# Down projection of a hybrid block: residual read by ScalarE's queue, four value buffers, rows ended one by one, norm weight before the norm

## The chip, the cores and the metric

The kernel runs on one core of one Trainium2 chip. TensorE multiplies matrices into PSUM banks, VectorE and ScalarE work element by element, GpSimd does some sums and stores, and SyncE, ScalarE and GpSimd issue DMAs between HBM and SBUF. Each engine takes its own instructions strictly in order and waits for the others by semaphores. The metric is the device time of one execution in microseconds. Before the change it is 1729.08 us, the median of three runs (1724.63 to 1731.36).

## The reference

A decoder block over 1024 tokens of 1024 channels, all in float32: two attention mixers, gates and an output projection, then a SwiGLU feed-forward of width 2816, and a last RMS norm. The change touches only the end, from the feed-forward's second product on:

```python
u = rms_norm(h, ffn_norm_g[layer])
h = h + swiglu(u, w_gate[layer], w_up[layer], w_down[layer])   # silu(u@w_gate) * (u@w_up) @ w_down
return rms_norm(h, final_norm_g)      # h * rsqrt(mean(h*h) + 1e-6) * final_norm_g
```

## The kernel before

**Products.** The down projection multiplies gated values (1024 tokens by 2816) by `w_down` (2816 by 1024). Both are cut into two by two blocks and multiplied with seven block products instead of eight (Strassen's method in Winograd's form), named in `PRODUCTS`: A00, S1, S2, S4, S3, A01, A11. Each runs over 11 blocks of 128 rows, so there are 77 steps. I number them 0 to 76, with step n = 11 i + p for product i and block p.

**One step.** A step needs a value tile (128x512, read back from HBM, where the feed-forward's first half left it: `fetch`) and a weight tile (128x512, in SBUF; in some products it is first made as a difference of two). Float32 is kept by splitting each into a rounded part and a rest (`split`): ScalarE casts the rounded part `oh`, VectorE subtracts it to get the rest `ol`. TensorE then does three products (L1372 to L1374) for each of four blocks of 128 tokens (`tb`), 12 matmuls of 128x512 a step. Four PSUM banks gather one product, one bank for each `tb`; two sets, `bx` and `by`, take turns. In the trace the banks of `bx` are called tp, tp, mm, mm.

**Rings.** The value tiles have a ring of two, `ar`; `oh` and `ol` have rings of six each, shared with the feed-forward's first half, which is three steps of two. A value buffer is free again when VectorE has taken the rest from it.

**Order.** The Python loop fetches step n+2, prepares step n+1 and multiplies step n. The instructions then pass a scheduler that gives each engine a fixed order of its own. On SyncE's queue it puts the eight reads of the residual (`hf`, 512 KB each, L1417) and eleven reads of weight blocks (`b10`, 256 KB each, L1289) among the first values of product A00, because their buffers are free by then.

**Ends.** When a product is complete its banks are kept (`kept`) or added to the residual rows `hf[t]` and squared (`settle`: t is one of eight blocks of 128 rows, c one of two halves of 512 columns). When both halves of `hf[t]` are complete, `finish` adds the two sums of squares, takes the reciprocal root (L168 to L181, with the root itself on ScalarE, L172), multiplies each half by the root and by the norm's weight in one VectorE instruction (L1400, L1402) and stores it. Rows t = 0 to 3 end after product A01, t = 4 to 7 at the very end. The last three steps (74 to 76) are written so that each `tb` runs through all three and is then settled:

```python
elif n == NS - 1:
    for tb in range(4):
        for m in range(NS - GRP, NS):
            step(m, (tb,))
        settle(tb + 4, 0, bx[tb], None)
        finish(tb + 4)
```

With rings of six the operands of step 76 can be cast only when step 73 is done, and the scheduler laid these steps out one after the other, all four banks in each.

## Time and profile before

| | |
|---|---|
| median of three runs | 1729.08 us |
| profiled execution, whole time | 1729.99 us |
| its span, first to last instruction | 1728.3 us |
| TensorE busy | 1648.4 us, 95% |
| VectorE busy | 1088.0 us, 63% |
| ScalarE busy | 769.7 us, 45% |
| GpSimd busy | 441.9 us, 26% |
| mean granted TensorE clock | 0.983 of full speed |

The busy share is an average over the whole run. The page's second part cuts the span into 40 slices of 43 us: TensorE reads 9 (90% or more) in nearly all of them, except the first, the 25th, the 36th (1512 to 1556 us) and the last, and these dips are where an engine waits for another. TensorE's records overlap: a 128x512 matmul is shown with 0.39 us, but the next one starts 0.23 us later. Idle time of an engine other than the one that is waited for costs nothing. The span leaves out 1.69 us that lie around it in the whole time.

### The profile page before, as it was taken

To read this page: it belongs to the slowest core of one execution; us is meant where nothing else is said; L and a number is where in the kernel's file an instruction comes from. 1 tells how busy PE (TensorE), PEld (TensorE's weight loads), DVE (VectorE), ACT (ScalarE), POOL (GpSimd) and SP (SyncE) were. 2 spreads that over 40 slices of the span, in tenths; PEclk is the share of its full clock that TensorE was granted. 3 is DMA by queue.
4 is the path that set the end of the run, shared out by engine and by line. 5 is a ranking of instruction groups with operands and counts; after the bars stand their busy time and mean duration, and the time that the engine had idled before them with its cause. 6 is when DMAs were issued, how large, how long until landed. Compare 5 with 4: busy or idle time off the path is not lost.

```text
span 1728.3 us, 25058 instructions
## 1 busy us (share of the span) xinstructions
PE 1648.4 (95%) x9025; PEld 1422.4 (82%) x9025; DVE 1088.0 (63%) x2148; ACT 769.7 (45%) x1644; POOL 441.9 (26%) x626
## 2 busy tenths in 40 slices
PE   5999999999999999999999997999999999989997
PEld 4888888888889988998878885788888888878885
DVE  8554545546349668888754248665655665766557
ACT  4334334334423257877854134433333333335444
POOL 4532323323122336656626110010010011100000
PEclk8999999999999999999999998999999999999998
DMA  6120211113213010100193420433223233763334
GB/s 209 46 80 25 80 43 44 49 44 95 85 71 99 17 31 12 49 16 20 29 313 125 167 98 37 134 123 122 92 97 116 92 103 105 253 231 95 98 97 146
DMA packets 150635, 163.68 MB, mean 95 GB/s; under 512 B 11616, under 2 KB 114048, under 8 KB 150512
## 3 DMA queue, kind: packets, MB, share of 16 engines
q1 hardware_dynamic: 139568, 129.62, 23.9%
q0 software_dynamic: 9760, 31.94, 4.8%
q8 instruction: 71, 1.16, 0.3%
q10 hardware_dynamic: 1184, 0.53, 0.1%
q14 instruction: 52, 0.43, 0.1%
HBM read 117.76 MB, written 44.30 MB: 94 GB/s over the span
## 4 chain that ended last, share of the span: by engine, by line
PE 80%; DVE 8%; issue 5%; ACT 3%; DMA 3%; POOL 2%; SPq 0%; DVEq 0%; ACTq 0%; POOLq 0%
PE mm L1140 8%; PE mm L1141 8%; PE mm L1142 8%; PE b L159 5%; PE b L160 5%; PE b L161 5%; PE b L927 3%; PE s L874 3%; PE mm L1372 3%; PE mm L1373 3%; PE mm L1374 3%; PE b L938 3%; PE s L159 2%; PE s L160 2%; PE s L161 2%
## 5 line engine op out<-in xcount | busy, mean ns | idle before, releaser
L1133 ACT ACTIVATE oh<-S 128x512 fp32r<-128x512 f32 x88 | 55.7, 633 | 138.9 <-PE mm L1141 138.3
L159 PE MATMUL b<-uh,mg_h 128*128 128x512 f32 x288 | 114.9, 399 | 0.7 <-ACT mg_st L337 0.7
L160 PE MATMUL b<-ul,mg_h 128*128 128x512 f32 x288 | 113.8, 395 | 0.0
L161 PE MATMUL b<-uh,mg_l 128*128 128x512 f32 x288 | 112.9, 392 | 0.0
L874 PE MATMUL s<-kN,qN 128*128 128x320 f32 (+5 forms) x384 | 98.8, 360 | 4.2 <-ACT p L891 3.3
L942 DVE TENSOR_TENSOR pl<-b,ph 128x512 fp32r<-128x512 f32 (+1 forms) x152 | 90.6, 613 | 12.3 <-ACT ph L941 11.2
L1351 ACT ACTIVATE oh<-ar 128x512 fp32r<-128x512 f32 x77 | 48.6, 632 | 106.5 <-PE mm L1373 72.8
L1352 DVE TENSOR_TENSOR ol<-ar,oh 128x512 fp32r<-128x512 f32 x77 | 53.3, 692 | 66.2 <-ACT oh L1351 62.6
L160 PE MATMUL b<-pw_l,uh 128*128 128x384 f32 x256 | 88.1, 344 | 6.5 <-DVE pw_l L269 6.5
L941 ACT ACTIVATE ph<-b 128x512 fp32r<-128x512 f32 (+1 forms) x152 | 80.2, 544 | 31.3 <-PE b L938 29.9
L891 ACT ACTIVATE p<-s,mn 128x640 f32<-128x640 f32 (+7 forms) x128 | 89.3, 703 | 7.6 <-DVE mn L885 2.5
L159 PE MATMUL b<-pw_h,uh 128*128 128x384 f32 x256 | 89.2, 348 | 1.8 <-ACT uh L218 1.2
L898 POOL TENSOR_TENSOR p<-p,sm 128x640 f32<-128x640 f32 (+3 forms) x64 | 89.2, 1414 | 2.5
L1133 ACT ACTIVATE oh<-raw 128x512 fp32r<-128x512 f32 x66 | 41.5, 632 | 108.3 <-PE mm L1141 104.7
L161 PE MATMUL b<-pw_h,ul 128*128 128x384 f32 x256 | 87.9, 343 | 1.4 <-DVE ul L219 1.4
L1373 PE MATMUL mm<-ol,oh 128*128 128x512 f32 x220 | 86.2, 392 | 0.0
L1374 PE MATMUL mm<-oh,ol 128*128 128x512 f32 x220 | 86.1, 391 | 0.0
L938 PE MATMUL b<-ident,p 128*128 128x128 f32 x528 | 82.5, 273 | 1.8 <-POOL p L895 1.2
L465 DVE TENSOR_REDUCE mn<-s 128x1 f32<-128x128 f32 (+7 forms) x64 | 46.0, 753 | 53.8 <-PE s L464 53.8
L1134 DVE TENSOR_TENSOR ol<-S,oh 128x512 fp32r<-128x512 f32 x88 | 59.6, 687 | 29.9 <-ACT oh L1133 25.6
L159 PE MATMUL s<-pw_h,uh 128*128 128x256 f32 (+1 forms) x256 | 75.9, 297 | 2.6 <-ACT xs L648 1.6
L927 PE MATMUL b<-ph,vN 128*128 128x256 f32 x264 | 75.1, 302 | 0.0
(432 smaller groups left out, 5188.9 us busy)
## 6 DMA issues: line engine op xcount, KB each, us to landing
raw<-in_w_gate_dram SPq DMA_DIRECT2D x22, 512.0 KB, 5.0
raw<-in_w_up_dram SPq DMA_DIRECT2D x22, 512.0 KB, 4.6
mg_raw<-in_w_in_dram SPq DMA_DIRECT2D x18, 512.0 KB, 4.6
mgd<-mg_st POOLq DMA_DIRECT2D x32, 256.0 KB, 3.7
sg<-mgd SPq DMA_DIRECT2D x16, 512.0 KB, 4.7
pw_raw<-in_w_in_dram SPq DMA_DIRECT2D x24, 256.0 KB, 4.2
b<-in_w_down_dram SPq DMA_DIRECT2D x22, 256.0 KB, 5.8
xt<-in_x_dram SPq DMA_DIRECT2D x8, 512.0 KB, 5.4
```

Of the source, the lines that this page charges most:

```text
L159: T.matmul(ps, ah, bh, start=(i == 0), stop=False)
L160: T.matmul(ps, ah, bl, start=False, stop=False)
L161: last = T.matmul(ps, al, bh, start=False, stop=(i == n - 1))
L874: T.matmul(s_[:, c], qN[:, 2 * hp + es[c * len(es) // 2], i * 128:(i + 1) * 128], kNs[br][:, v, g, c0:c0 + cw], start=(v == 0), stop=(v == 1))
L927: T.matmul(o, lhsT, rhs, start=(done == 0), stop=(done == total - 1))
L938: T.transpose(tp[:, 2 * (b - b0) + e], p[:, e, b * 128:(b + 1) * 128], ident)
L1133: A.activation(wh, src, AF.Copy)
L1140: T.matmul(ps, w[0][:, k], b[0][:, k], start=(first and k == 0), stop=False, **kw)
L1141: T.matmul(ps, w[0][:, k], b[1][:, k], start=False, stop=False, **kw)
L1142: T.matmul(ps, w[1][:, k], b[0][:, k], start=False, stop=(k == 3), **kw)
L1373: T.matmul(ps, ah[:, ts], wl, start=False, stop=False, **kw)
L1374: T.matmul(ps, al[:, ts], wh, start=False, stop=(p == HF - 1), **kw)
```

## The change

Four things are changed in the down projection, as the diff shows.

1. The residual's rows `hf[t]` are read by ScalarE's queue, one behind a value cast of steps 12, 14, 16 and 18 (t = 0 to 3) and 34, 36, 38 and 40 (t = 4 to 7). The norm's weight `gO` is read there behind the cast of step 23. `issue_after` fixes that place in ScalarE's order.
2. Values alternate between `ar` and two buffers `arf` in the memory of the feed-forward's raw weights, so a ring of four. Fetches run four steps ahead, preparing two.
3. The operands of step 73 go to four tiles of another ring, `u2d`, whose values are used up by then; so those of steps 74 to 76 fit into the rings of six together.
4. `settle` multiplies the rows by the norm's weight after they have been squared; `finish` has only the reciprocal root left, on VectorE for the first half and on ScalarE for the second.

```diff
@@ -1342,24 +1342,37 @@
         i, p = divmod(n, HF)
         if PRODUCTS[i][3]:
             load_block(PRODUCTS[i][3], p)
-        raw_a[n] = dn.tile([128, 512], F32, name="ar", bufs=2)
+        if n % 2:
+            raw_a[n] = ffr.tile([128, 512], F32, name="arf", tag="raw", bufs=2)
+        else:
+            raw_a[n] = dn.tile([128, 512], F32, name="ar", bufs=2)
         nc.sync.dma_start(raw_a[n], hh_dram[PRODUCTS[i][0]][p])
 
-    def split(src):
-        h = ff.tile([128, 512], R, name="oh", bufs=6)
-        l = ff.tile([128, 512], R, name="ol", bufs=6)
-        A.activation(h, src, AF.Copy)
+    def split(src, spare):
+        if spare:
+            h, l = [dr.tile([128, 512], R, name="u2" + v, tag="u2d", bufs=4) for v in "hl"]
+        else:
+            h = ff.tile([128, 512], R, name="oh", bufs=6)
+            l = ff.tile([128, 512], R, name="ol", bufs=6)
+        cast = A.activation(h, src, AF.Copy)
         V.tensor_sub(l, src, h)
-        return h, l
+        return (h, l), cast
 
     def prepare(n):
         i, p = divmod(n, HF)
         _, nm, make, _, _ = PRODUCTS[i]
-        a = split(raw_a.pop(n))
+        a, cast = split(raw_a.pop(n), n == NS - 1 - GRP)
         w = BW[nm][p]
         if make:
             V.tensor_sub(w, BW[make[0]][p], BW[make[1]][p])
-        ops[n] = a + split(w)
+        ops[n] = a + split(w, n == NS - 1 - GRP)[0]
+        if i in (1, 3) and 1 <= p < 9 and p % 2:
+            t = p // 2 + (0 if i == 1 else 4)
+            with tc.issue_after(cast.ins):
+                nc.scalar.dma_start(hf[t], hx_dram[t])
+        elif i == 2 and p == 1:
+            with tc.issue_after(cast.ins):
+                nc.scalar.dma_start(gO, bcast_rows(final_norm_g, D))
 
     def step(n, tbs):
         i, p = divmod(n, HF)
@@ -1391,32 +1404,29 @@
             V.tensor_add(hc, hc, part)
         sq = ff.tile([128, 512], F32, name="S", bufs=3)
         A.activation(sq, hc, AF.Square, accum_out=ssq[:, t, c:c + 1])
+        V.tensor_mul(hc, hc, gO[:, c * 512:c * 512 + 512])
 
     def finish(t):
         V.tensor_add(ssq[:, t, 0:1], ssq[:, t, 0:1], ssq[:, t, 1:2])
         r = rsqrt(dr, [128, 1], ssq[:, t, 0:1], 1.0 / D, "fin")
         rows = slice(t * 128, (t + 1) * 128)
         h0, h1 = hf[t][:, 0:512], hf[t][:, 512:1024]
-        V.scalar_tensor_tensor(h0, h0, r, gO[:, 0:512], op0=OP.mult, op1=OP.mult)
+        V.tensor_scalar(h0, h0, r, None, op0=OP.mult)
         nc.sync.dma_start(out[rows, 0:512], h0)
-        V.scalar_tensor_tensor(h1, h1, r, gO[:, 512:1024], op0=OP.mult, op1=OP.mult)
+        A.activation(h1, h1, AF.Copy, scale=r)
         nc.sync.dma_start(out[rows, 512:1024], h1)
 
-    for n in range(2):
+    for n in range(4):
         fetch(n)
     prepare(0)
+    prepare(1)
     keep = {}
     for n in range(NS):
         i, p = divmod(n, HF)
+        if n + 4 < NS:
+            fetch(n + 4)
         if n + 2 < NS:
-            fetch(n + 2)
-        if n == HF:
-            nc.sync.dma_start(gO, bcast_rows(final_norm_g, D))
-        if i in (2, 4) and p < 4:
-            t = p + (0 if i == 2 else 4)
-            nc.sync.dma_start(hf[t], hx_dram[t])
-        if n + 1 < NS:
-            prepare(n + 1)
+            prepare(n + 2)
         if n < NS - GRP:
             step(n, range(4))
         elif n == NS - 1:
```

**SyncE's queue, the values of steps 7 to 10.** `ar` and `arf` are value tiles (A00d_11162 is step 7, A00d_11163 step 8, A00d_11165 step 10), `hf` the residual's rows, `b` the weight blocks. Before:

```order
L1417 DMA hf_15391<-hxd_11233 128x1024
L1346 DMA ar<-A00d_11162 128x512
L1417 DMA hf_15392<-hxd_11234 128x1024
L1417 DMA hf_15393<-hxd_11235 128x1024
L1417 DMA hf_15394<-hxd_11236 128x1024
L1417 DMA hf_15395<-hxd_11237 128x1024
L1417 DMA hf_15396<-hxd_11238 128x1024
L1417 DMA hf_15397<-hxd_11239 128x1024
L1289 DMA b_0_15379<-in_w_down_dram 128x512
L1346 DMA ar<-A00d_11163 128x512
```

Now:

```order
L1349 DMA ar<-A00d_11163 128x512
L1289 DMA b_0_15379<-in_w_down_dram 128x512
L1289 DMA b_1_15380<-in_w_down_dram 128x512
L1349 DMA arf<-A00d_11164 128x512
L1289 DMA b_2_15381<-in_w_down_dram 128x512
L1289 DMA b_3_15382<-in_w_down_dram 128x512
L1289 DMA b_4_15383<-in_w_down_dram 128x512
L1289 DMA b_5_15384<-in_w_down_dram 128x512
L1289 DMA b_6_15385<-in_w_down_dram 128x512
L1289 DMA b_7_15386<-in_w_down_dram 128x512
L1289 DMA b_8_15387<-in_w_down_dram 128x512
L1349 DMA ar<-A00d_11165 128x512
```

The reads of the residual are gone from this queue; step 8's values (the first row) stand ahead of all weight blocks, step 9's behind two of them and step 10's behind nine.

**TensorE's and VectorE's last work.** The banks tp_15399, tp_15400, mm_15401 and mm_15402 belong to the rows hf4 to hf7. Operands 17245 and 17240 are step 74's, 17266 and 17261 step 75's and 17287 and 17282 step 76's in the new order; 17275 and 17270 are step 76's in the old. TensorE's last twelve matmuls before:

```order
L1372 MATMUL tp_15399<-oh_17275,oh_17270 128x512
L1372 MATMUL tp_15400<-oh_17275,oh_17270 128x512
L1372 MATMUL mm_15401<-oh_17275,oh_17270 128x512
L1372 MATMUL mm_15402<-oh_17275,oh_17270 128x512
L1373 MATMUL tp_15399<-ol_17276,oh_17270 128x512
L1374 MATMUL tp_15399<-oh_17275,ol_17271 128x512
L1373 MATMUL tp_15400<-ol_17276,oh_17270 128x512
L1374 MATMUL tp_15400<-oh_17275,ol_17271 128x512
L1373 MATMUL mm_15401<-ol_17276,oh_17270 128x512
L1374 MATMUL mm_15401<-oh_17275,ol_17271 128x512
L1373 MATMUL mm_15402<-ol_17276,oh_17270 128x512
L1374 MATMUL mm_15402<-oh_17275,ol_17271 128x512
```

Now:

```order
L1385 MATMUL mm_15401<-oh_17287,oh_17282 128x512
L1386 MATMUL mm_15401<-ol_17288,oh_17282 128x512
L1387 MATMUL mm_15401<-oh_17287,ol_17283 128x512
L1385 MATMUL mm_15402<-oh_17245,oh_17240 128x512
L1386 MATMUL mm_15402<-ol_17246,oh_17240 128x512
L1387 MATMUL mm_15402<-oh_17245,ol_17241 128x512
L1385 MATMUL mm_15402<-oh_17266,oh_17261 128x512
L1386 MATMUL mm_15402<-ol_17267,oh_17261 128x512
L1387 MATMUL mm_15402<-oh_17266,ol_17262 128x512
L1385 MATMUL mm_15402<-oh_17287,oh_17282 128x512
L1386 MATMUL mm_15402<-ol_17288,oh_17282 128x512
L1387 MATMUL mm_15402<-oh_17287,ol_17283 128x512
```

Before, the last twelve matmuls are step 76 on all four banks. Now the bank of hf6 is complete nine matmuls before the end, and only the bank of hf7 is worked on after that (of hf4 and hf5, 17 and 15 before the end). VectorE before, from the first row that waits for the last matmuls:

```order
L1388 TENSOR_TENSOR hf4_15394<-hf4_15394,tp_15399 128x512
L1388 TENSOR_TENSOR hf5_15395<-hf5_15395,tp_15400 128x512
L1388 TENSOR_TENSOR hf6_15396<-hf6_15396,mm_15401 128x512
L1388 TENSOR_TENSOR hf7_15397<-hf7_15397,mm_15402 128x512
L1396 TENSOR_TENSOR ssq_15398<-ssq_15398 128x1 x2
L168 TENSOR_SCALAR fin_a_17292<-ssq_15398 128x1
L168 TENSOR_SCALAR fin_a_17318<-ssq_15398 128x1
L1396 TENSOR_TENSOR ssq_15398<-ssq_15398 128x1 x2
L173 RECIPROCAL fin_r_17293<-fin_t_17294 128x1
```

Now, up to the row behind the last bank's addition:

```order
L1401 TENSOR_TENSOR hf6_15396<-hf6_15396,mm_15401 128x512
L1407 TENSOR_TENSOR hf5_15395<-hf5_15395,qB22l_15378 128x512
L1410 TENSOR_TENSOR ssq_15398<-ssq_15398 128x1
L168 TENSOR_SCALAR fin_a_17305<-ssq_15398 128x1
L173 RECIPROCAL fin_r_17306<-fin_t_17307 128x1
L1407 TENSOR_TENSOR hf6_15396<-hf6_15396,qB22l_15378 128x512
L168 TENSOR_SCALAR fin_a_17332<-ssq_15398 128x1
L1410 TENSOR_TENSOR ssq_15398<-ssq_15398 128x1
L176 SCALAR_TENSOR_TENSOR fin_t_17307<-fin_r_17306,fin_a_17305 128x1
L1401 TENSOR_TENSOR hf7_15397<-hf7_15397,mm_15402 128x512
L173 RECIPROCAL fin_r_17333<-fin_t_17334 128x1
```

The addition of hf7 stands behind the weight's multiplication of hf6 (L1407), and the reciprocal roots of hf4 and hf5 are worked out around it.

**ScalarE's casts of steps 71 to 73.** The names with 17169 and 17174 are step 71's before, with 17171 and 17176 now. Before, steps 71 to 73 follow in turn:

```order
L1351 ACTIVATE oh_17169<-ar_17144 128x512
L1351 ACTIVATE oh_17174<-b00_5_12214 128x512
L172 ACTIVATE fin_t_17046<-ssq_15398,epst_86 128x1
L1351 ACTIVATE oh_17192<-ar_17167 128x512
L1351 ACTIVATE oh_17197<-b00_6_12215 128x512
L172 ACTIVATE fin_t_17064<-ssq_15398,epst_86 128x1
L1351 ACTIVATE oh_17215<-ar_17190 128x512
L1351 ACTIVATE oh_17220<-b00_7_12216 128x512
```

Now u2h are the casts of step 73:

```order
L1357 ACTIVATE oh_17171<-arf_17123 128x512
L1357 ACTIVATE oh_17176<-b00_5_12214 128x512
L172 ACTIVATE fin_t_17051<-ssq_15398,epst_86 128x1
L1357 ACTIVATE u2h_17217<-arf_17169 128x512
L1357 ACTIVATE u2h_17222<-b00_7_12216 128x512
L1357 ACTIVATE oh_17194<-ar_17146 128x512
L1357 ACTIVATE oh_17199<-b00_6_12215 128x512
```

The casts of step 73 stand ahead of those of step 72.

## Rows read from the trace of the kernel before

**Rows 1.** Stages: busy us of PE, PEld, DVE, ACT, POOL; clock, DMA share, GB/s.
```profile
1500.00:1530.00 30.00, 25.06 (x100) 20.23 (x100) 20.49 (x34) 7.67 (x13) 3.24 (x6) 0.90 1.02 389
1530.00:1560.00 30.00, 30.00 (x131) 24.74 (x131) 23.71 (x38) 15.57 (x28) 0.00 (x0) 0.98 0.35 105
...
1620.00:1650.00 30.00, 30.00 (x134) 24.87 (x133) 18.85 (x30) 15.43 (x30) 0.00 (x0) 1.00 0.32 97
```

**Rows 2.** TensorE's timeline around 1520 us: start, length, line, tiles, [idle].
```profile
1519.32 0.39 PE L1373 MATMUL mm<-ol,oh 128*128 128x512 f32 x1
1519.55 0.39 PE L1374 MATMUL mm<-oh,ol 128*128 128x512 f32 x1
1524.88 1.22 PE L1372 MATMUL tp<-oh 128*128 128x512 f32 x2 [4.94 <-ACT oh L1351]
...
1531.51 0.39 PE L1373 MATMUL tp<-ol,oh 128*128 128x512 f32 x1
```

**Rows 3.** ScalarE's timeline: the last raw weights' cast, those of steps 7 and 8.
```profile
1481.72 0.63 ACT L1133 ACTIVATE oh<-raw 128x512 fp32r<-128x512 f32 x1 [1.19 <-DMA qB11h<-in_w_down_dram]
...
1514.39 0.63 ACT L1351 ACTIVATE oh<-ar 128x512 fp32r<-128x512 f32 x1 [4.31 <-PE mm L1373]
...
1523.67 0.63 ACT L1351 ACTIVATE oh<-ar 128x512 fp32r<-128x512 f32 x1 [8.13 <-DMA ar<-A00d]
```

**Rows 4.** Chain of waits, two DMA pieces: start, us, what.
```profile
1506.44 7.84 DMA ar<-A00d
1514.36 9.21 DMA ar<-A00d
```

**Rows 5.** SyncE's DMA issues, 1503 to 1526 us: start, time to issue.
```profile
1503.68 1.85 SPq L1417 DMA_DIRECT2D hf<-hxd  x2
1506.44 0.32 SPq L1346 DMA_DIRECT2D ar<-A00d  x1
1506.86 3.96 SPq L1417 DMA_DIRECT2D hf<-hxd  x6
...
1514.36 0.32 SPq L1346 DMA_DIRECT2D ar<-A00d  x1
...
1522.34 3.54 SPq L1289 DMA_DIRECT2D b<-in_w_down_dram  x6
```

**Rows 6.** DMA issues: count, KB each, median us to landing.
```profile
hf<-hxd SPq DMA_DIRECT2D x8, 512.0 KB, 9.9
...
ar<-S1d SPq DMA_DIRECT2D x11, 256.0 KB, 2.6
...
ar<-A11d SPq DMA_DIRECT2D x11, 256.0 KB, 2.7
```

**Rows 7.** All engines in order of time, the end of the kernel.
```profile
1714.43 1.29 DVE L1388 TENSOR_TENSOR hf<-hf,tp 128x512 f32<-128x512 f32 x2 [4.77 <-PE tp L1374]
...
1715.36 0.39 PE L1374 MATMUL mm<-oh,ol 128*128 128x512 f32 x1
...
1717.00 0.63 ACT L1393 ACTIVATE S<-hf 128x512 f32<-128x512 f32 x1
...
1717.94 0.35 DVE L173 RECIPROCAL fin_r<-fin_t 128x1 f32<-128x1 f32 x2
...
1718.85 0.75 DVE L1400 SCALAR_TENSOR_TENSOR hf<-hf,fin_r,qB22l 128x512 f32<-128x512 f32 x1
...
1724.39 0.75 DVE L1402 SCALAR_TENSOR_TENSOR hf<-hf,fin_r,qB22l 128x512 f32<-128x512 f32 x1
...
1725.17 0.33 SPq L1403 DMA_DIRECT2D out_dram<-hf  x1
```

**Rows 8.** VectorE's timeline: the rest of step 4's values is taken.
```profile
1502.59 0.68 DVE L1352 TENSOR_TENSOR ol<-ar,oh 128x512 fp32r<-128x512 f32 x1
```

**Rows 9.** ScalarE's queue at the start: a DMA issued there.
```profile
0.80 0.41 ACTq L346 DMA_DIRECT2D gB<-in_attn_norm_g_dram  x1
```

**Rows 10.** VectorE's groups with shapes apart: one operand tensor, a scalar.
```profile
L387 DVE TENSOR_SCALAR ropeC<-ropeC 128x512 f32<-128x512 f32 x1 | 0.4, 420 | 0.0
```

## The prediction, before the change was run

> **What bounds the kernel now.** I read the page first: TensorE is busy nearly everywhere, so only the dips count. The table by stages [rows 1] puts the one dip of the down projection at 1500 to 1530 us: TensorE 25.06 of 30 us, granted clock 0.90, while the DMA engines are full (share 1.02, 389 GB/s). In the next 30 us TensorE has no gap, the DMA share is 0.35, and VectorE, the next busiest, has 23.71 of 30. TensorE's timeline then shows the hole itself [rows 2]: matmuls start 0.23 us apart, the last of step 7 at 1519.55, so the next could start at 1519.78; it starts at 1524.88. That is 5.10 us. It resumes at half speed: from 1524.88 to 1531.51 there are 16 matmuls, 6.63 us where 16 x 0.23 = 3.68 would do, 2.95 lost at 1.2 instead of 2.4 GHz. The hole costs 8.05 us.
>
> Its cause is in the chain of waits and in SyncE's queue. Step 8's cast waited 8.13 us for its values [rows 3]; these were issued at 1514.36 and took 9.21 us [rows 4]. They were late twice. Six residual reads and one weight block stand ahead of them on SyncE, which issues in order [rows 5]; and the residual's 4.2 MB filled the DMA engines, where such a value read otherwise lands after 2.6 us [rows 6].
>
> The second loss is the end. The last matmul ends at 1715.75 = E [rows 7]; four banks are added, squared and scaled then, all at once, and the last scaled half leaves VectorE at 1725.14. The span ends at 1728.3, which is E + 12.55, and 3.16 us of it are the last store.
>
> **Hole (-8.05 us).** The eight residual reads leave SyncE's queue and stand behind casts of steps 12 to 18 and 34 to 40, over 20 us later (step 12's casts begin with step 10, at 1525.2; the first read went out at 1503.68 [rows 5]). Step 8's values need the buffer of step 4, which VectorE empties from 1502.59 on [rows 8]; so they go out at about 1503.3 instead of 1514.36. Even with the worst landing shown, 9.21 us, they are there at 1512.5, and TensorE wants them cast by 1519.78, so landed by 1518.5. What is late next? Seven weight blocks (0.59 us to issue each, 3.54 for six [rows 5]) stand between step 9's values and step 10's. From the buffer of step 5 (about 1506.4) I reach 1510.6 for step 10, and with 9.21 us 1519.8; it is wanted, two steps of 2.72 us after step 8 and 1.2 for the casts, at 1524.0. Between 1500 and 1530 us the DMA engines moved 11.7 MB (389 GB/s x 30); without the residual 7.5 MB are left, 19 us of work. VectorE had 44.2 us of work in these 60 us [rows 1], and has 52 now: 85%, no bound. The reads of steps 1 and 3 go to the feed-forward's raw buffers, the last of which is cast at 1481.72 [rows 3] and free some 1.5 us later; SyncE waits there for that long at most, with weight blocks behind it that step 11 wants first, at 1527.9: nothing. GpSimd's queue is not touched. I take the whole 8.05; ends: nothing, if the wait moves on unchanged, and 8.05.
>
> The Trainium skill has a rule that speaks against this part ("DMA: Bandwidth & Descriptors", section "Issuing engines are not separate DMA queues"): DMAs from any engine share the same 16 DMA engines, and another issuing engine saves only the time to issue. By the rule alone the queue brings nothing but some 6 us of SyncE's time, and the sum would be that of rival 2. The DMA share of 1.02 agrees with it; what decides here is that the reads also come later.
>
> **The reads where they are now (0).** Nine DMA issues on ScalarE, 0.41 us each [rows 9], or 0.66 as on a full queue (six in 3.96 [rows 5]): 3.7 to 5.9 us of ScalarE, never more than one in two steps. A step's casts may begin when the step three before it is done, two steps (5.44 us) ahead, and take 1.2: 4.2 us of cover. One 512 KB read each 5.44 us adds 96 GB/s to the 105 shown, half of 389 [rows 1]; values are now asked for four steps (10.9 us) ahead. Without that cover an issue costs 0.41 to 0.66.
>
> **End (-3.85 us).** TensorE's order now finishes the banks of hf4, hf5 and hf6 17, 15 and 9 matmuls before E (3.9, 3.4, 2.0 us). I walk VectorE's new order with before's durations: an addition or multiplication starts 0.60 after the one ahead (two in 1.29), small ones 0.09 (ten from the reciprocals to the first scaled half in 0.91), a square takes 0.63 plus 0.19 to read its sum [rows 7]. hf6's multiplication by the weight runs into E + 0.48, and hf7's addition behind it ends at E + 1.16 (before, its square started at E + 1.25). Its square ends at 1.9, its multiplication and sum at 2.6, its root, behind ScalarE's halves of hf4 and hf5, at 3.4, its reciprocal at 4.2. VectorE's halves are now one-tensor instructions, 0.42 [rows 10] for 0.75; ScalarE's I take at 0.63, as its casts. The last half is out at E + 5.2, SyncE's queue adds 0.35 since its last four stores now crowd, and with the store's 3.16 the end is E + 8.7 instead of 12.55. The norm weight moves 16 multiplications ahead of the root: 12 lie in stages where VectorE is 63 to 79% busy [rows 1] and replace eight longer ones, four are in the walk. Ends of this term: if nothing overlapped, four halves less (4 x 0.66) and four multiplications more (4 x 0.60) gain 0.2; if only hf7's own chain were left behind E, about 6.2 with its store, it gains 6.3. I take the walk.
>
> **Step 72 (+0.2 us).** ScalarE's order has step 73's casts ahead of step 72's, and step 73's values can only be asked for when VectorE has emptied step 71's buffer. From the start of step 69 as zero: step 71 is cast, VectorE, busy with the ends of rows 0 to 3, gets to it at about 3.1; the read lands 2.7 later [rows 6] at 5.8; four casts end at 8.05; TensorE wants step 72 at three steps, 8.16. Nothing hides a later landing. Behind the waiting cast are steps 72 to 76, and TensorE waits for all of them. Bounds: nothing, and with the 9.21 us of a full queue 6.4 of waiting plus 2.95 at the lower clock, 9.35. The nearest row is the same read's median, 2.7, so I take 0.2.
>
> **Sum.** Against the profiled execution's own 1729.99 us (span 1728.3, 1.69 around it): 1729.99 - 8.05 - 3.85 + 0.2 = 1718.3. The median of the runs lies 0.9 lower, so I forecast 1717.4 us.
>
> **Rivals.**
> 1. A new wait takes part of the hole: step 72 comes 3.4 us late, and TensorE resumes at the lower clock: + 3.4 + 2.95 = 1723.7. For it: no cover, and VectorE's load there. Against: this read's 2.7 us on an otherwise half-empty queue; the stores of rows 0 to 3 now stand behind the last values.
> 2. The reads are only moved: the DMA engines stay full and the hole stays, now behind weight blocks; the end alone is gained: 1729.08 - 3.85 + 0.2 = 1725.4. For it: 7.5 MB are still left in that stage. Against: six microseconds of margin at step 8. It is the rule of the skill cited above, carried to its end.
> 3. The rows do not end in turn in fact: VectorE's strict order, with cross waits for ScalarE's roots, gives the gain back, and only the hole goes: 1729.08 - 8.05 = 1721.0, with the other small term 1721.2.
> 4. Slower: a residual read holds ScalarE until the DMA ring takes it. It decides from a hold of 4.2 us, ScalarE's cover; beyond that each of the nine places stops TensorE and drops its clock. At 5 us: 9 x (0.8 + 2.95) = 33.8, 1751 us. For it: SyncE took 3.96 us for six on a full queue. Against: this is 0.66 each, and the rings are a third full then.
>
> **Chances.** Forecast 0.66, its own range 1714 to 1721 (runs of the kernel before differ by 6.7 us, and the end's term is soft). Rivals: first 0.13, second 0.07, third 0.08, fourth 0.06. The range of 1713.5 to 1724 takes in rivals 1 and 3 and leaves out 2 and 4, and the forecast's tails. About 0.5%, 8.6 us, is what a measurement of this kernel can tell from no change: below 1720.4 is faster. That holds for nine tenths of the forecast and part of the third rival, 0.64; slower is rival 4 and a remainder, 0.07; the rest is 0.29.
>
> **What would show it.** Hole: no gap over 1 us on TensorE between 1480 us and the end, granted clock 1.00 in 1500 to 1530, step 8's values issued about 11 us earlier, casts waiting for steps' ends instead of DMAs. Reads: about 10 us or less to landing on ScalarE's queue, DMA share of 0.5 to 0.7 where they run. End: last matmul to the end of the span 8.7 us. I am wrong if ScalarE's casts of step 8, 10 or 73 wait for a DMA while TensorE stands, or if VectorE is still multiplying and scaling all four rows behind E.

## The result, and the profile after

The changed kernel takes 1718.55 us (median of six runs, 1715.96 to 1721.26), the kernel before 1729.51 (six runs, 1724.63 to 1732.60). The ratio is 0.9944, with a 95% interval of 0.9930 to 0.9957: 0.56% faster, and clear of no change. 1717.4 was forecast. The profiled execution was the slowest of the six: 1721.26 us, span 1719.3.

To compare two spans I cut each at two instants which every profile has. The first is the start of ScalarE's last cast of raw feed-forward weights (L1133, in [rows 3] 1481.72). The second is E, the end of the last matmul. In front of the first lies work that the change does not touch; between them lies the down projection, called the stretch here; behind E lies the end.

| | last raw cast | E | stretch | end |
|---|---|---|---|---|
| before | 1481.72 | 1715.75 | 234.03 | 12.55 |
| after | 1483.48 | 1709.43 | 225.95 | 9.87 |
| difference | +1.76 | | -8.08 | -2.68 |

The work in front was 1.76 us late in this execution, before anything changed had run. In all the profiles of this study the cast falls between 1478.73 and 1484.77, whatever the kernel; the scatter between runs of one kernel is of that size. So I argue with the stretch and the end, and leave the front out.

The stages after (columns: start and end; busy us of PE, PEld, DVE, ACT, POOL; clock, DMA share, GB/s), to set beside [rows 1]:

```profile
1500.00:1530.00 30.00, 30.00 (x134) 24.86 (x133) 28.63 (x46) 12.87 (x24) 3.24 (x6) 1.00 0.82 286
1530.00:1560.00 30.00, 30.00 (x134) 24.87 (x133) 21.91 (x33) 14.72 (x28) 0.00 (x0) 1.00 0.53 165
```

TensorE has no idle time in them, the granted clock is 1.00, and the DMA engines have room. VectorE is now the engine nearest to a limit: 28.63 of 30 us. TensorE's timeline shows no gap anywhere from 1485 us to E.

SyncE's issues there (start, length), to set beside [rows 5]:

```profile
1505.06 0.33 SPq L1349 DMA_DIRECT2D ar<-A00d  x1
1505.43 0.95 SPq L1289 DMA_DIRECT2D b<-in_w_down_dram  x2
1508.07 0.33 SPq L1349 DMA_DIRECT2D arf<-A00d  x1
1508.44 3.74 SPq L1289 DMA_DIRECT2D b<-in_w_down_dram  x7
```

ScalarE's casts of steps 8 and 9, and the first residual read on its queue (ACTq), to set beside [rows 3]:

```profile
1516.07 0.63 ACT L1357 ACTIVATE oh<-ar 128x512 fp32r<-128x512 f32 x1 [1.57 <-PE mm L1386]
...
1518.79 0.63 ACT L1357 ACTIVATE oh<-arf 128x512 fp32r<-128x512 f32 x1 [1.57 <-PE mm L1386]
...
1526.95 0.63 ACT L1357 ACTIVATE oh<-ar 128x512 fp32r<-128x512 f32 x1 [1.57 <-PE mm L1386]
1526.95 0.34 ACTq L1372 DMA_DIRECT2D hf<-hxd  x1
```

Step 8's values (1505.06) now go out 11 us ahead of their cast (1516.07). Less the 1.76 us that the front is late, that is 1503.30, the moment that the prediction gave. The casts wait for TensorE to release operand tiles, not for a DMA. The first residual read is issued by ScalarE in 0.34 us, and the cast beside it starts at the same instant. The eight reads land after 4.1 us (median), where they took 9.9 in [rows 6]:

```profile
hf<-hxd ACTq DMA_DIRECT2D x8, 512.0 KB, 4.1
```

The end, all engines in order of time, to set beside [rows 7]:

```profile
1709.04 0.39 PE L1387 MATMUL mm<-oh,ol 128*128 128x512 f32 x1
...
1710.11 0.68 DVE L1401 TENSOR_TENSOR hf<-hf,mm 128x512 f32<-128x512 f32 x1
...
1710.88 0.63 ACT L1406 ACTIVATE S<-hf 128x512 f32<-128x512 f32 x1 [1.43 <-DVE fin_t L180]
...
1711.74 0.33 SPq L1415 DMA_DIRECT2D out_dram<-hf  x1
...
1712.92 0.28 ACT L172 ACTIVATE fin_t<-ssq,epst 128x1 f32<-128x1 f32 x1
...
1713.23 0.16 DVE L173 RECIPROCAL fin_r<-fin_t 128x1 f32<-128x1 f32 x1
...
1713.76 1.33 ACT L1416 ACTIVATE hf<-hf,fin_r 128x512 f32<-128x512 f32 x2 [0.56 <-DVE fin_r L181]
...
1714.16 0.15 DVE L181 TENSOR_TENSOR fin_r<-fin_r,fin_t 128x1 f32<-128x1 f32 x1
...
1714.35 0.49 DVE L1414 TENSOR_SCALAR hf<-hf,fin_r 128x512 f32<-128x512 f32 x1
...
1715.70 0.40 SPq L1417 DMA_DIRECT2D out_dram<-hf  x1
```

E is 1709.04 + 0.39 = 1709.43. hf7's addition starts 0.68 behind it, its square at 1.45, its root at 3.49, ScalarE's last half (the second of two at 1713.76) is made at E + 5.66, and its store goes out at E + 6.27. The span ends 3.60 later, 2.6 to the landing and about 1 behind it; the whole is called the store's time here, as in the prediction. The first store of the last four rows, at 1711.74, matters too, as will be seen: from it to the end of the span are 7.56 us.

### The profile page after: what moved, and what is told of

Its sections match the earlier page's. It is cut to its first block, busy times and chain, and to the rows that moved or that the text cites. A ratio compares the mean times of both kernels' runs of the same rounds, so it can differ in the third digit from the quotient of the medians.

```text
span 1719.3 us, 25072 instructions
## 1 busy us (share of the span) xinstructions
PE 1647.1 (96%) x9025; PEld 1423.3 (83%) x9025; DVE 1090.3 (63%) x2156; ACT 775.1 (45%) x1652; POOL 441.5 (26%) x626
## 4 chain that ended last, share of the span: by engine, by line
PE 82%; DVE 7%; issue 5%; ACT 3%; POOL 2%; DMA 1%; SPq 0%; ACTq 0%; POOLq 0%; DVEq 0%
PE mm L1140 8%; PE mm L1141 8%; PE mm L1142 8%; PE b L159 5%; PE b L160 5%; PE b L161 5%; PE s L874 3%; PE b L927 3%; PE mm L1386 3%; PE mm L1385 3%; PE mm L1387 3%; PE b L938 3%; PE s L159 2%; PE s L161 2%; PE s L160 2%
## 5 line engine op out<-in xcount | busy, mean ns | idle before, releaser
L1133 ACT ACTIVATE oh<-S 128x512 fp32r<-128x512 f32 x88 | 55.7, 633 | 142.2 <-PE mm L1141 140.1
L1133 ACT ACTIVATE oh<-raw 128x512 fp32r<-128x512 f32 x66 | 41.5, 632 | 108.3 <-PE mm L1141 105.9
L160 PE MATMUL s<-pw_l,uh 128*128 128x256 f32 (+1 forms) x256 | 74.3, 290 | 0.0
L161 PE MATMUL s<-pw_h,ul 128*128 128x256 f32 (+1 forms) x256 | 74.0, 289 | 0.0
```

The costliest lines, as they stand in the source:

```text
L160: T.matmul(ps, ah, bl, start=False, stop=False)
L161: last = T.matmul(ps, al, bh, start=False, stop=(i == n - 1))
L1133: A.activation(wh, src, AF.Copy)
```

## The experiments

Theory: the hole came from the residual reads, which stood ahead of the values and filled the DMA engines at that moment; moving them later removes it, and rows that end in turn with the weight ahead shorten the end. Rivals: the issuing queue or the depth of the rings is what counts; at the end, VectorE's order or the stores are what ends last. Each run is timed in rounds beside the kernel before on its own chip. "Stretch" and "end" are worked out from each run's profile as in the table above.

| run | median us | ratio to before, 95% interval | stretch | end |
|---|---|---|---|---|
| 1 reads moved alone | 1720.09 | 0.9935 to 0.9960 | 225.90 | 12.48 |
| 2 deeper rings alone | 1721.76 | 0.9944 to 0.9969 | 227.09 | 12.47 |
| 3 reads early, ScalarE | 1724.15 | 0.9961 to 0.9984 | 230.37 | 9.89 |
| 4 reads late, SyncE | 1719.25 | 0.9928 to 0.9956 | 225.95 | 9.92 |
| 5 rows together | 1720.69 | 0.9942 to 0.9970 | 225.91 | 12.86 |
| 6 weight last | 1720.83 | 0.9940 to 0.9967 | 225.95 | 12.39 |
| 7 weight with root | 1718.63 | 0.9923 to 0.9953 | 225.95 | 8.79 |
| 8 the same, last store by ScalarE | 1716.52 | 0.9914 to 0.9940 | 225.95 | 8.88 |
| 9 as 7, one store a row | 1716.21 | 0.9908 to 0.9932 | 225.95 | 8.97 |
| 10 as 9, row 4 on ScalarE | 1718.30 | 0.9922 to 0.9952 | 225.95 | 9.42 |
| 11 changed kernel again | 1720.55 | 0.9931 to 0.9958 | 225.96 | 9.97 |
| 12 small stores | 1716.29 | 0.9910 to 0.9947 | 225.96 | 9.36 |

Stretch and end repeat to 0.1 us, the medians to about 2: runs 7 to 12 are told apart by their profiles, not by their medians.

**Run 1, the reads' place alone.** The kernel before with this edit (shortened; the weight's read moves in the same way):

```diff
+        if i in (1, 3) and 1 <= p < 9 and p % 2:      # in prepare
+            with tc.issue_after(cast.ins):
+                nc.scalar.dma_start(hf[t], hx_dram[t])
-            nc.sync.dma_start(hf[t], hx_dram[t])      # in the loop
```

> The kernel before with one part of the change: the eight residual reads and the norm weight's read go out on ScalarE's queue behind the casts of the same steps as in the changed kernel; rings of two values, the end as before. Theory A (the reads' place alone made the hole): step 8's values go out near 1503.5 instead of 1514.36, TensorE has no gap over 1 us around 1520, granted clock 1.00 in 1500 to 1530, and the time falls by the 8.05 us of the hole, from 1729.5 to about 1721.5; the end stays 12.55 us behind the last matmul. Theory B (two values in flight are too few as well): a gap of 2 to 5 us stays or moves to steps 9 to 11, where weight blocks stand ahead of the values: 1724 to 1729.

```profile
1500.00:1530.00 30.00, 30.00 (x134) 24.85 (x133) 25.48 (x42) 14.07 (x25) 2.17 (x4) 1.00 0.75 252
```

No gap, clock 1.00, DMA share 0.75, and the stretch is as short as the whole change makes it. Theory A: with two value buffers the hole is gone as soon as the reads stand elsewhere. The end stays at 12.48.

**Run 2, the rings alone.** The kernel before with four values in flight, operands two steps ahead, reads early on SyncE as before (shortened):

```diff
-        raw_a[n] = dn.tile([128, 512], F32, name="ar", bufs=2)
+        raw_a[n] = (ffr.tile(..., name="arf", tag="raw", bufs=2) if n % 2
+                    else dn.tile(..., name="ar", bufs=2))
-            fetch(n + 2); prepare(n + 1)
+            fetch(n + 4); prepare(n + 2)
```

> The kernel before with another part alone: four values in flight and operands made ready two steps ahead; the residual reads stay on SyncE's queue, early, and the end stays as before. SyncE's order has step 8's values ahead of all eight reads, step 9's ahead of six, step 10's behind all. Theory A (what counts is that a value is asked for long enough ahead of its cast): DMA engines full in 1500 to 1530 as before, share about 1.0, reads and values landing in 8 to 10 us, and yet no gap over 1 us on TensorE: step 10's values go out near 1512, land by 1521.5 and are wanted at 1524. About 1721.5. Theory B (while the residual fills the DMA engines a value is late wherever it stands): the gap moves to step 10 or 11, 3 to 6 us with the lower clock behind it: 1725 to 1729.

The stage:

```profile
1500.00:1530.00 30.00, 29.15 (x129) 23.81 (x128) 24.20 (x39) 12.29 (x23) 3.25 (x6) 1.00 1.03 392
```

SyncE, the issue of step 10's values:

```profile
1511.46 0.32 SPq L1349 DMA_DIRECT2D ar<-A00d  x1
```

ScalarE, their cast:

```profile
1521.88 0.63 ACT L1354 ACTIVATE oh<-ar 128x512 fp32r<-128x512 f32 x1 [4.97 <-DMA ar<-A00d]
```

TensorE's only gap, at step 11:

```profile
1527.67 1.19 PE L1375 MATMUL mm<-oh 128*128 128x512 f32 x4 [0.85 <-ACT oh L1354]
```

The DMA engines are as full as before (1.03, 392 GB/s). Step 10's values go out at 1511.46 and are cast at 1521.88, 10.4 us later, near the 1512 and 1521.5 expected; one gap of 0.85 is left: theory A. The stretch loses 1.14 of the 8.08. So each of two parts of the change removes the hole nearly alone, and their gains do not add.

The gap that is left is no wait for a DMA either. ScalarE's order in this run has step 11's casts behind evictions of A00's banks, which wait for TensorE's step 10:

```profile
1525.50 1.09 ACT L1384 ACTIVATE sl<-tp 128x512 f32<-128x512 f32 x2 [2.46 <-PE tp L1377]
1526.47 0.63 ACT L1354 ACTIVATE oh<-arf 128x512 fp32r<-128x512 f32 x1
```

In the changed kernel the first of these casts stands ahead of the evictions:

```profile
1524.23 0.63 ACT L1357 ACTIVATE oh<-arf 128x512 fp32r<-128x512 f32 x1 [1.57 <-PE mm L1386]
```

**Run 3, the reads early on ScalarE.** The changed kernel without `issue_after`: the reads stand in the loop, on `nc.scalar`, as early as before.

> The changed kernel with the eight residual reads still on ScalarE's queue, but not held back: they stand among the casts of steps 5 to 8, some 15 us ahead of where the change has them. Theory A (cover decides): DMA share near 1.0 in 1500 to 1530, the reads' landing near 10 us again instead of 4.1, ScalarE held for 0.4 to 0.7 us by each; values asked for 11 us ahead of their casts still come in time: 1718.6, within 1. Theory B (only holding the reads back freed the DMA engines): values of steps 10 to 12 late, a gap of 3 to 5 us on TensorE, 1723 to 1727.

ScalarE around the reads:

```profile
1508.69 7.29 ACTq L1425 DMA_DIRECT2D hf<-hxd  x2
1516.10 0.63 ACT L1357 ACTIVATE oh<-arf 128x512 fp32r<-128x512 f32 x1 [6.86 <-DMA hf<-hxd]
```

TensorE's two longest gaps:

```profile
1517.31 0.73 PE L1378 MATMUL tp<-oh 128*128 128x512 f32 x2 [0.87 <-ACT oh L1357]
...
1531.44 1.20 PE L1378 MATMUL mm<-oh 128*128 128x512 f32 x4 [1.80 <-ACT oh L1357]
```

The stage, and a stretch around the longer gap of TensorE alone:

```profile
1500.00:1530.00 30.00, 28.34 (x121) 21.90 (x119) 22.07 (x36) 10.24 (x19) 3.25 (x6) 1.00 1.02 388
```

```profile
1529.00:1535.00 6.00, 4.20 (x19) 1.00 0.48 137
```

ScalarE's evictions of A00's banks, and step 11's first cast:

```profile
1528.29 1.09 ACT L1387 ACTIVATE sl<-tp 128x512 f32<-128x512 f32 x2 [4.48 <-PE tp L1380]
...
1530.21 0.65 ACT L1357 ACTIVATE oh<-arf 128x512 fp32r<-128x512 f32 x1
```

Theory B's price (a stretch 4.4 us longer, in the 1723 to 1727 expected), but not its wait: no gap of TensorE is for a late value. Two other things make it up, which neither theory had sized.

The first is a wait in ScalarE's queue. The row of 7.29 us is two issues, one of 0.46 at 1508.69 and one of 0.33 at 1515.65; what lies between is no issuing. By the semaphores in the trace, the program lets a read go only when the earlier DMA that signals the same semaphore has landed, and the DMAs of SyncE and ScalarE here share eight of them:

| read on ScalarE | issued, length | waits for the read issued at | which landed at |
|---|---|---|---|
| sixth | 1515.65, 0.33 | 1505.75 | 1515.63 |
| seventh | 1517.10, 0.33 | 1506.45 | 1517.08 |
| eighth | 1518.94, 0.33 | 1508.32 | 1518.92 |

While a read waits, so does the cast behind it, 6.86 and 2.12 us. That is rival 4 of the prediction at the place where the reads were before, with another reason: landings that take 8.8 us (median) on full DMA engines. TensorE loses 2.2 us by it: the last matmul of step 6 starts at 1516.05 and the first of step 10 at 1526.67, 10.62 later, where 0.23 and three steps of 2.72 make 8.39.

The second is ScalarE's order, as in run 2. The longest gap, 1.80 at step 11, comes because step 11's casts stand behind the evictions, which wait 4.48 for TensorE; the value itself had been asked for at 1520.86 and landed 6.2 later. This makes up the other 2.2 us, so the price of the early reads on ScalarE is shown as about half of the 4.4.

The Trainium skill ("DMA: Bandwidth & Descriptors", section "Issuing engines are not separate DMA queues", cited in the prediction) adds that the time to initiate a DMA is usually small beside the DMA itself. The trace agrees: none of the eight issues takes over 0.66 us, and the reads land after 7.0 to 12.1. What costs is the wait ahead of an issue.

**Run 4, late but on SyncE.** The changed kernel; the read waits on SyncE's queue for a one-column copy into its tile (the weight's read likewise):

```diff
-            with tc.issue_after(cast.ins):
-                nc.scalar.dma_start(hf[t], hx_dram[t])
+            A.activation(hf[t][:, 0:1], a[0][:, 0:1], AF.Copy)
+            nc.sync.dma_start(hf[t], hx_dram[t])
```

> The changed kernel with the nine reads back on SyncE's queue, at the same late steps: each waits there for a one-column copy on ScalarE into its own tile (overwritten by the read), behind the first cast of steps 12, 14, ... Theory A (the moment counts, not the issuing queue): SyncE waits now and then for ScalarE, values stand behind it for at most a step of 2.72 us out of 10.9 of cover: 1718.6, within 0.7, reads landing in about 4 us, no gap on TensorE. Theory B (SyncE's queue itself was in the way): values behind a waiting read come late, gaps around steps 15 to 22 and 37 to 44, 1721 or more.

```profile
hf<-hxd SPq DMA_DIRECT2D x8, 512.0 KB, 3.6
```

Stretch 225.95, the same to the hundredth as with ScalarE's queue, landing 3.6: theory A. The moment counts, the queue does not, as long as the DMA engines have room. That DMAs run on the same engines whoever issues them is what the Trainium skill says ("DMA: Bandwidth & Descriptors", section "Issuing engines are not separate DMA queues"); at the late moment the trace agrees with it. At the early moment the queue did make a difference: with the same rings and reads the stretch is 227.09 with SyncE's (run 2) and 230.37 with ScalarE's (run 3), part of it by ScalarE's order.

**Run 5, rows ended together.** The changed kernel with `spare = False` in `split`: the order of TensorE's last steps goes back to that of before, the rest stays.

> The changed kernel without the two spare operand tiles for step 73: TensorE's order goes back to ending the four last banks together, in the last 9 matmuls. Reads, rings, norm weight first and ScalarE's halves stay. E is the end of the last matmul; the span ended at E + 12.55 before and at E + 9.87 in the changed kernel. Theory A (rows in turn carry about half of the gain at the end): additions run to E + 1.2, four multiplications by the weight to 3.6, roots and halves to 6.9, the stores 4.2 more: E + 11.1, 1719.8 us. Theory B (VectorE's own order is the limit and the turn brings nothing): E + 9.9, 1718.6.

ScalarE's last half (E = 1705.54):

```profile
1713.08 0.72 ACT L1417 ACTIVATE hf<-hf,fin_r 128x512 f32<-128x512 f32 x1 [0.33 <-DVE fin_r L181]
```

SyncE's first and last issue:

```profile
1710.76 0.33 SPq L1416 DMA_DIRECT2D out_dram<-hf  x1
...
1714.27 0.51 SPq L1418 DMA_DIRECT2D out_dram<-hf  x1
```

The end is 12.86, not 11.1: more than theory A foresaw, and no better than before. The last half is made at E + 8.3 (6.9 expected, 9.4 before), but the eight stores go out within 3.5 us of each other, and the last takes 4.13. From the first of them to the end of the span are 7.64 us, where the changed kernel has 7.56.

**Run 6, weight last.** The changed kernel without the multiplication in `settle`, and with both halves scaled by root and weight on VectorE, as before.

> The changed kernel with the norm weight applied last, as before: no multiplications in advance, both halves of every row on VectorE with root and weight in one instruction (0.66 apart). Rows still end in turn. Theory A (weight first and ScalarE's halves gain nothing by themselves, since four multiplications stand on VectorE's path instead): hf7's addition starts 0.1 behind E instead of 0.68, eight long halves run from E + 0.9 to 6.4, stores to E + 9.7: 1718.4. Theory B (they carry the rest of the gain): E + 11 or more, 1719.8 or more.

VectorE (E = 1708.11), hf7's addition, the first and the last long half:

```profile
1708.43 0.68 DVE L1401 TENSOR_TENSOR hf<-hf,mm 128x512 f32<-128x512 f32 x1
...
1710.59 0.75 DVE L1413 SCALAR_TENSOR_TENSOR hf<-hf,fin_r,qB22l 128x512 f32<-128x512 f32 x1
...
1716.64 0.74 DVE L1415 SCALAR_TENSOR_TENSOR hf<-hf,fin_r,qB22l 128x512 f32<-128x512 f32 x1
```

12.39: theory B. The eight long halves only start at E + 2.5 and end at E + 9.3. It is not a clean removal of one part: TensorE's order changes with it, and the banks of hf4 to hf6 end 7, 5 and 3 matmuls ahead of E instead of 17, 15 and 9. With that reserve, runs 5 and 6 say that the two parts at the end gain only as a pair: 12.86 and 12.39 one at a time, 12.55 with none, 9.87 with both.

**Runs 7 and 8, weight and root in one, for the last halves only.**

```diff
-        V.tensor_mul(hc, hc, gO[...])
+        if c or t < 4: V.tensor_mul(hc, hc, gO[...])
-        V.tensor_scalar(h0, h0, r, None, op0=OP.mult)
+        V.scalar_tensor_tensor(h0, h0, r, gO[:, 0:512], ...)   # rows 4 to 7
-        nc.sync.dma_start(out[rows, 512:1024], h1)             # run 8 only
+        (nc.scalar if t == 7 else nc.sync).dma_start(out[rows, 512:1024], h1)
```

> The changed kernel with one edit at the end: the four halves that the last product adds (rows 4 to 7) are not multiplied by the weight ahead; VectorE applies root and weight in one instruction there (0.66 instead of 0.60 + 0.40), ScalarE scales the other halves as in the changed kernel. Theory A (hf7's chain stood behind VectorE's multiplications, 0.68 us before its addition and 0.8 before its sum): addition at E + 0.2, square to 1.8, root 2.65, scaled by 4.0, last store issued at 4.4: E + 7.9, 1716.6. Theory B (the stores' queue is the limit): SyncE's last four issues still 0.5 apart, E + 9.4 or more, 1718.1.

> As the run before it in this list (weight and root together for the last four halves), and the very last half is stored from ScalarE's queue, which has just made it, instead of SyncE's. Theory A (SyncE's crowded queue cost 0.61 us between the last half and its issue): E + 7.4, 0.5 less, 1716.1. Theory B (the store itself takes longer when several are under way, whoever issues it): no more than 0.2 less than without this.

Run 7's addition and last half of hf7 (E = 1704.71):

```profile
1705.05 0.68 DVE L1401 TENSOR_TENSOR hf<-hf,mm 128x512 f32<-128x512 f32 x1
...
1708.71 0.75 DVE L1418 SCALAR_TENSOR_TENSOR hf<-hf,fin_r,qB22l 128x512 f32<-128x512 f32 x1
```

SyncE's last issue there:

```profile
1709.88 0.40 SPq L1419 DMA_DIRECT2D out_dram<-hf  x1
```

Run 8's last two issues, ScalarE's and, for hf7's other half, SyncE's (E = 1707.62):

```profile
1712.38 0.37 ACTq L1421 DMA_DIRECT2D out_dram<-hf  x1
1712.40 0.33 SPq L1419 DMA_DIRECT2D out_dram<-hf  x1
```

GB/s in run 7, in 40 slices from 1704.5 to 1713.5 us:

```profile
GB/s 0 0 0 0 0 64 391 382 401 419 428 246 0 0 0 137 391 410 419 410 391 383 428 428 392 382 410 419 419 382 401 419 355 18 0 0 0 0 0 0
```

The end falls to 8.79, about half way between 7.9 and 9.4. The last half is made at E + 4.75, 0.9 earlier, but the store still takes 3.62. In run 8 both last issues come some 0.4 earlier (E + 4.76 and 4.78), and the span still ends 4.1 behind them (ScalarE's lands last, after 3.0 against 2.6): the end is 8.88, nothing is gained, theory B. The last six halves' bytes run without a pause for 4 us in run 7, which would be the reason; no run removes them there. By its median run 8 is 2.1 us faster than run 7, but its end is not, and the stretch is the same.

**Runs 9 to 11.** Run 9 is run 7 with rows 4 to 6 stored whole; run 10 also gives both halves of row 4 to ScalarE, the last of them with the weight ahead; run 11 is the changed kernel beside them.

> As the run with weight and root together at the end, and rows 4 to 6 are stored whole (512 KB, one issue) instead of in two halves; row 7 still in two. In that run the last half was made at E + 4.75, its store issued at 5.17 and done 3.62 later, where a store after an uncrowded queue took 3.1. Theory A (the crowd of stores ahead costs about 0.9 of this: 0.42 in SyncE's queue and 0.5 in the store): last issue E + 5.1 (two remain side by side), store 3.2, E + 8.3. Theory B (the bytes under way count, not the number of stores): E + 8.7 to 8.9 as there.

> As the run before it in this list, and row 4 is scaled by ScalarE alone, its last half multiplied by the weight in VectorE's idle time ahead of E; VectorE then has three weight-and-root instructions behind E instead of four, and hf7's addition has none ahead of it. Theory A (VectorE's order ahead of hf7's root is still what ends last): addition at E + 0.1 instead of 0.34, last half at E + 4.4 instead of 4.75, end 0.3 earlier than in that run, about E + 8.0. Theory B (ScalarE, with five halves and two squares, becomes the limit): hf7's square starts later than E + 1.2, no gain. The time of the whole: 1718.6 less 1.6 to 1.9, about 1716.9.

> The changed kernel as it is, timed beside the two runs above on the same chip, so that they are compared with it directly: 1718.6 within 1.5; the span from the last cast of the feed-forward's weights to the last matmul 225.95 us, and from there to the end 9.87. What differs between two executions of it lies ahead of that cast, 1478.8 to 1483.8 in the profiles so far.

SyncE's last store in run 9 (E = 1705.93):

```profile
1711.10 0.41 SPq L1423 DMA_DIRECT2D out_dram<-hf  x1
```

hf7's square in run 10 (E = 1704.68):

```profile
1706.18 0.61 ACT L1406 ACTIVATE S<-hf 128x512 f32<-128x512 f32 x1
```

Run 9: issue at E + 5.17 as in run 7, store 3.80, an end of 8.97 where theory B had 8.7 to 8.9 and theory A 8.3: fewer stores with the same bytes help nothing. Run 10: hf7's addition comes early (E + 0.04) as planned, but its square only at E + 1.50, behind two halves and a root on ScalarE: theory B, 0.45 worse. Run 11 repeats the changed kernel: stretch 225.96, end 9.97. Its median of 1720.55 is 1.95 above the 1718.6 that was expected within 1.5, and its front is the latest of all, 1484.77 in the profile. Run 9 has the lowest interval of all (0.9908 to 0.9932, against 0.9931 to 0.9958 for run 11 beside it); 1.0 us of this is its shorter end; by the profiles the rest lies in front of the down projection, where the edits change nothing.

**Run 12, small stores.**

```diff
-        nc.sync.dma_start(out[rows, 0:512], h0)
+        nc.sync.dma_start(out[rows, 0:cs], h0[:, 0:cs])   # cs = 128 in rows 4 to 7,
                                                           # likewise h1 in rows 4 to 6
```

> The changed kernel with less to store at the end: of the last eight half rows seven store only 128 of their 512 columns (the rest of the output stays unwritten there); the very last half is stored whole. All other instructions and their order stay. In the changed kernel the eight stores moved 2.10 MB without a pause at about 405 GB/s, 5.2 us, and the last one, issued at E + 6.27, was done 3.60 later. Theory A (the last store waits for the bytes ahead of it): the last half is still made at E + 5.66, but SyncE's issues are 0.33 instead of 0.41 each and the store takes 3.1 as after a queue with room: E + 9.1 at most 9.4, that is 0.5 to 0.8 less. Theory B (issue and store cost what they cost after four instructions in a row, bytes or not): E + 9.9.

Bytes moved, and GB/s in 40 slices, in the changed kernel from 1711 to 1720 us:

```profile
GB/s 0 0 0 0 0 0 9 373 400 428 401 382 410 419 428 373 401 419 410 410 400 392 410 428 401 391 410 410 428 364 28 0 0 0 0 0 0 0 0 0
DMA packets 1152, 2.10 MB, mean 233 GB/s; under 512 B 128, under 2 KB 128, under 8 KB 1152
```

The same in run 12 from 1708 to 1718.1 us:

```profile
GB/s 0 0 0 0 0 0 0 0 0 0 0 0 0 0 0 160 100 164 96 24 233 43 219 0 0 154 106 195 65 219 41 381 422 235 0 0 0 0 0 0
DMA packets 1152, 0.72 MB, mean 71 GB/s; under 512 B 128, under 2 KB 1024, under 8 KB 1152
```

Run 12's last issue (E = 1708.74):

```profile
1714.95 0.38 SPq L1419 DMA_DIRECT2D out_dram<-hf  x1
```

In the changed kernel the stores run without a pause near 405 GB/s for 5.2 us. In run 12 they are 0.72 MB with pauses, in as many packets (1152); the last half is made at E + 5.66 all the same, its store is issued at E + 6.21 and done 3.15 later instead of 3.60. The end is 9.36, in theory A's range. The issues are 0.47 apart instead of 0.50, so that of SyncE's 0.6 us hardly anything goes back to the bytes.

## Why the prediction was right, point by point

The median lies 1.15 us above the forecast. The end's miss, 1.17, is the one term that is off by more than 0.2.

**The hole (-8.05).** Right in size: the stretch is 8.08 shorter. Run 1 shows that the reads' place does it. The prediction gave the rings no share of their own; run 2 shows that they would have done 6.9 of it alone (the other 1.1 is ScalarE's order, not a DMA). The wait for a landing that run 3 shows is in the hole too: between 1500 and 1535 us of the kernel before, SyncE's weight issues waited 7.2 us in six waits for residual reads to land, with the values behind them. In the changed kernel no issue of SyncE's waits for one there. The moved reads and the rings overlap, and the sum holds because the prediction counted the hole once.

**The reads on ScalarE (0).** Right for where they stand: 0.34 us each. The price that I put on an issue with full DMA engines, 0.66, is not far off either: 0.33 to 0.66 in run 3, 0.32 to 1.02 for the reads of the kernel before. What I left out is the wait ahead of an issue until an earlier DMA has landed: 6.5 us between two issues in run 3. Rows that merge issues hide it. The 3.54 for six blocks in [rows 5], which I read as 0.59 to issue each, are issues of 0.33 with such waits between them. What saves the change is the moment: a DMA share of 0.53 and reads that land after 4.1. Rival 4 was nearer than its 0.06 in the hold, but not in its reason or its price. How full a ring is, as it argued, no view shows; and it charged 2.95 for the clock at a gap of 0.8, where gaps of 0.85 and 1.80 cost none (runs 2 and 3).

**Rival 2 and the skill's rule.** The reads do share the DMA engines whoever issues them (runs 3 and 4). The rival failed at its next step: full DMA engines alone do not make the hole. In run 2 they are full, and TensorE waits for no value, since values are asked for early enough.

**VectorE.** I reckoned 52 us of work in 60 (87%, not the 85% that I wrote); it has 28.63 + 21.91 = 50.5, but 95% in the first half, without a wait of TensorE.

**Step 72 (+0.2).** No gap: 0. No cast there waits for a DMA. Rival 1 did not come.

**The end (-3.85).** The mechanism was right, the size was not: -2.68, an end of 9.87 instead of 8.7. The step that failed is "the last half is out at E + 5.2, SyncE's queue adds 0.35, and with the store's 3.16". Measured are 5.66, 0.61 and 3.60. Of the 1.17 us, 0.44 is the store. I took its time from the kernel before, whose stores left 0.66 apart; now they leave 0.50 apart, and 256 KB at 405 GB/s need 0.65. Run 12 shows this: with little ahead of it the store takes 3.15. A further 0.26 is SyncE's issues, 0.41 long instead of 0.33. The last 0.46 is VectorE's and ScalarE's walk. hf7's root starts nearly as reckoned, at E + 3.49 for 3.4. Behind it I counted small instructions 0.09 apart, but where each needs the one before they start 0.2 apart (reciprocal 1713.23, the next of its row 1713.43), hf6's half stands among hf7's, and a half takes ScalarE 0.71 instead of 0.63.

The three are shares of one chain, not gains that wait to be taken. The stores' bytes run without a pause, so a last half that came earlier alone would have waited longer in its store. What the walk left out is this second bound: the first store and eight times 0.65 us of bytes, 7.56 us from the issue at E + 2.31 to the end (7.64 in run 5). Run 12 takes the bytes away, and the last half's chain alone then ends 0.5 earlier.

**Rival 3.** The rows do end in turn; its 1721.2 is close to run 5 and run 6 (1720.7 and 1720.8), where one half of the pair is missing.

**The sum.** 1729.99 - 8.08 - 2.68 + 1.76 + 0.27 (the time around the span, 1.96 instead of 1.69) = 1721.26, the profiled time. By medians the change is worth 10.96, the stretch and the end 10.76.

What stays open is why the work in front of the down projection ends up to 6 us earlier or later from one profile to the next; no run was made for it.

## What to carry to other kernels

Before pricing a moved DMA, ask what the DMA engines carry at the new moment, and which earlier DMA has to land before the program lets this one go: the issue itself took 0.3 to 1.0 us even on full engines, the wait ahead of it up to 6.5. On SyncE such a wait holds up other DMAs, on ScalarE its compute. Look at the engines' order before a gap is put down to a DMA: two of the gaps here were casts that stood behind evictions. When two edits each cure the same wait, count it once. At the end of a kernel the bytes of the last stores are a term of their own: results made faster than 256 KB in 0.65 us queue up behind each other, so that the first store's time matters as much as the last result's.

## What the runs showed that I had not expected

- A short gap did not cost the clock: after TensorE's gaps of 0.85 us (run 2) and 1.80 us (run 3) the granted clock stayed 1.00 in the rows that cover them, 2.4 GHz, and after four matmuls 0.26 apart the next started 0.23 apart; behind the gap of 4.94 us in [rows 2] there were 16 matmuls at about half that speed, most of them 0.43 apart, with a granted clock of 0.50 (1.2 GHz) from 1524.9 to 1528.0 us.
- A DMA that waits for an earlier one to land holds up the compute of the engine that issues it: a cast on ScalarE stood for 6.86 us (run 3).
- Issuing the last stores 0.4 us earlier, one of them on ScalarE itself, moved nothing: the ends are 8.79 (run 7) and 8.88 (run 8) behind E.
